# A second transformer block: some weight remainders formed by an accumulating DMA, the residual scaled later and on VectorE, heads normed token tile by token tile, convolution taps queued

## The chip, the cores and the metric

One core of a Trainium2 chip runs the whole program. The engines are PE (TensorE), DVE (VectorE), ACT (ScalarE), POOL (GpSimd) and SP, whose queue here only issues DMAs. The metric is the device time of one execution in microseconds; lower is better.

## The reference

Two blocks follow one another on 512 tokens of width 1024. The first is a mixer, a cross attention and a convolutional feed-forward network; nothing in it changes. The second block, cut to what matters:

```python
h = rms_norm(x, norm1_g)
q, k, v, glu_a, glu_b = split(h @ w_in)          # 8 heads of 64; glu parts 512 wide
q, k = rms_norm per head (gains q_norm_g, k_norm_g)
attn = stick_breaking_attention(q, k, v)         # strictly causal, weights in log space
c = glu_a * sigmoid(glu_b)
c = causal_depthwise_conv(c)                     # 31 taps
c = silu(layer_norm(c))
x = x + concat([attn, c]) @ w_out
x = x + (silu(conv3(gate)) * val) @ w_down       # gate, val = split(rms_norm(x) @ w_up)
```

Here `x` is the first block's output, which ends in an RMS norm of its own (gain `final_norm_g`).

## The kernel before

Every product is made of three: both operands are split into a high part (rounded to the fp32r type that PE reads) and a low part, the remainder, and `mm3` adds high by high, high by low and low by high. Activations lie with features on partitions, 512 tokens on the free axis.

Weights come in 105 planned units of 128 x 2048 values (1 MB) plus three early ones. `prep` loads a unit into `raw`, casts it to `whi` on ACT (L195) and subtracts on DVE to get `wlo` (L196). `raw`, `whi` and `wlo` have two buffers each, so a unit's parts can be formed only when the unit two before it has been used up. In this text a unit has its number in the plan: 60, 61, 62 and 64 are the four column blocks of the gated part (`glu(0)` to `glu(3)`), 63 the second half of the keys, 65 and 66 the values, 67 to 70 the output projection. The three early units (all of the queries, half of the keys) are split ahead of time into slots E, F and G.

`mov_stage` multiplies 128-token tiles by a unit of 512 columns; it fills two pairs of PSUM banks (`pp`) weight half by weight half, so all four token tiles end together. `heads` then norms the heads for two tiles at a time: ACT squares, DVE sums (L731), POOL computes the inverse root (L737 to L740), DVE multiplies (L741), PE transposes (L745), ACT and DVE split the result. Between the products and this norming `heads` calls `gated(2)` or `gated(3)`, which queues the 48 products of a `glu` and a run of taps.

A tap is one DVE instruction on 128 x 512 values (L832). There are 120, in one chain: `conv` orders each behind the one before with `issue_after`. The first block's last norm is applied to the residual `h` by four POOL instructions (L871) before the attention.

The attention goes through pieces (hp, n): head pair 0 to 3, key step 0 to 2. `sticks` forms the scores on PE, then Abs, Exp and Ln on ACT, a maximum-and-add on DVE and a split; `breaks` adds the sums of the blocks behind on PE and takes Exp on ACT (L803); `gather` multiplies by the values. `conv_norm` is the layer norm and Silu of the convolution, and `attended` the half of the output projection that reads the heads.

No engine's order is written by hand: a scheduler places the instructions of each engine when the kernel is built, within the order of the code and the `issue_after` ties, and ACT table loads are put in after that. On the chip each engine goes through its own list in that order.

Of the kernel before, what the change touches and what calls it, by code (L numbers as in the profile page):

```python
# [57 lines left out]


PLAN, EARLY = _plan()  # L60

_SMALL = {}
_n = 0
# [12 lines left out]
def block_kernel(  # L76
# [36 lines left out]
    def col(n):  # L113
        return tp.tile([P, n], F32, tag=f"col{n}", name=f"col{n}", bufs=6 if n == 16 else 8)
# [27 lines left out]
    def over2(ap, n=2):  # L142
        return ap.unsqueeze(1).to_broadcast([P, n, ap.shape[-1]])
# [24 lines left out]
    def half(name, a, b, dt=F32R):  # L168
        return part(slot(name, dt), a, b)
# [4 lines left out]
    def prep(pieces=((0, 8),), before=None, between=None, early=None, slots=None):  # L174

        i = state["next"] if early is None else len(PLAN) + early
        if i == len(PLAN) and early is None:
            return
        if early is None:
            state["next"] += 1  # L180
        _, kind, place = (PLAN + EARLY)[i]
        n = place[2] * 256 if kind == "dwn" else UNIT
        raw = wp.tile([P, UNIT], F32, tag="raw", name="raw")
        hi = slot(slots[0]) if slots else wp.tile([P, UNIT], F32R, tag="whi", name="whi")
        lo = slot(slots[1]) if slots else wp.tile([P, UNIT], F32R, tag="wlo", name="wlo")
        for a, b in pieces:
            cs = slice(a * n // 8, b * n // 8)
            if before:
                before(a, b)
            sp.dma_start(out=raw[:, cs], in_=wts[i][:, cs])  # L190
        for a, b in pieces:
            cs = slice(a * n // 8, b * n // 8)
            if between:
                between(a, b)
            act.copy(hi[:, cs], raw[:, cs])  # L195
            dve.tensor_tensor(lo[:, cs], raw[:, cs], hi[:, cs].bitcast(F32), ALU.subtract)  # L196
        if kind == "hlf":
# [24 lines left out]
    def mov_stage(xh, xl, nt, early=()):  # L222

        pts = [pair() for _ in range((nt + 1) // 2)]
        early = list(early)
        for half in range(2):
            wh, wl = early.pop(0) if early else weights()
            for kk in range(4):
                k = 4 * half + kk
                for t in range(nt):  # L230
                    out = pts[t // 2][:, t % 2, :]
                    st = slice(t * P, (t + 1) * P)
                    mm3(out, xh[:, k, st], xl[:, k, st], wh[:, kk, :], wl[:, kk, :],
                        k == 0, k == KC - 1)
        return pts
# [6 lines left out]
    def par(name, i=0, n=1):  # L242
        o = _SMALL[name][0] + i
        return sm[:, o : o + n]
# [443 lines left out]
    def glu(i):  # L688
        pt = sta_unit(ph, pl)
        if i == 0:  # L690
            norms()
        ab = v3(t4(), 2, 512)
        dve.tensor_tensor(ab, pt, over2(rb2), ALU.mult)
        sig = act.activation(ab[:, 1, :], ab[:, 1, :], AF.Sigmoid)
        if i == 3:
            with tc.issue_after(sig.ins):
                act.preload_act_table_set(tables)
        dve.tensor_tensor(cc[:, i, 30:542], ab[:, 0, :], ab[:, 1, :], ALU.mult)  # L698

    rb2 = rb3 = None  # L700

# [14 lines left out]

    rr, rr2 = keep("rr"), keep("rr2")

    def heads(name, gain, sc, between, early=()):
        gc = col(1)  # L720
        dve.tensor_scalar(gc, par(gain), sc, None, ALU.mult)
        pts = mov_stage(ph, pl, NT, early)
        dst = [half(name + "0", 4, T), half(name + "1", 4, T)]
        between()
        for i in range(2):
            src = pts[i].rearrange("p a (b d) -> p (a b) d", d=HD)
            qn = norm2[:, 2 * i : 2 * i + 2, :]
            heads16 = qn.rearrange("p a (b d) -> p (a b) d", d=HD)
            act.activation(qn, pts[i], AF.Square)
            ms = col(16)  # L730
            dve.tensor_reduce(ms, heads16, AX.X, ALU.add)  # L731
            ms2 = ms.rearrange("p (a b) -> p a b", a=2)

            def per_token(c):
                return c[:, 2 * i : 2 * i + 2].unsqueeze(2).to_broadcast([P, 2, 8])

            pool.tensor_tensor(ms2, ms2, per_token(rr2), ALU.mult)  # L737
            pool.tensor_scalar(ms, ms, EPS, None, ALU.add)
            pool.tensor_tensor(ms, ms, mhalf[:, :16], ALU.pow)  # L739
            pool.tensor_tensor(ms2, ms2, per_token(rr), ALU.mult)  # L740
            dve.tensor_tensor(heads16, src, ms.unsqueeze(2).to_broadcast([P, 16, HD]), ALU.mult)  # L741
            tr = pair().rearrange("p a (b c) -> p (a b) c", b=2)
            for t in range(2):
                for hp in range(4):
                    pe.transpose(tr[:, hp, t * P : (t + 1) * P], qn[:, t, hp * P : (hp + 1) * P], ident)  # L745
            ts = slice(2 * i * P, (2 * i + 2) * P)
            scale_split(dst[0][:, :, ts], dst[1][:, :, ts], tr, gc)
        return dst
# [56 lines left out]
    def gather(hp):  # L805

        o = single(0)
        for n in range(3):
            for a in reversed(STEPS[n]):
                for e in range(2):  # L810
                    hs = slice(e * HD, (e + 1) * HD)
                    vs = slice(hp * P + e * HD, hp * P + (e + 1) * HD)
                    pe.matmul(o[hs, a * P :], v2[:, a, vs], taken(hp, n)[:, e, cols_of(a)],  # L813
                              start=a == 3, stop=a == 0, skip_group_check=True)
        copy_split(qT[0][:, hp, :], qT[1][:, hp, :], o)


    done = [0] * 4
    tap = None

    def conv(n, *chunks):

        nonlocal tap
        for _ in range(n):
            for i in chunks:
                k = done[i]
                done[i] += 1
                if k == 0:
                    identity(cv[:, i, :], cc[:, i, 30:542], scale=par("dw_w", 4 * 30 + i),
                             bias=par("dw_b", i))  # L830
                with tc.issue_after(tap.ins) if tap else nullcontext():
                    tap = dve.scalar_tensor_tensor(  # L832
                        cv[:, i, :], cc[:, i, k : k + 512], par("dw_w", 4 * k + i), cv[:, i, :],
                        ALU.mult, ALU.add)

    norm2 = half("D1", 4, T, F32)
    glu(0)
    split_early(2)
    conv(10, 0)
    turns = {1: ((20, 0, 1),), 2: ((10, 1, 2),), 3: ((20, 2), (30, 3))}  # L840

    def gated(i):
        glu(i)
        for n, *chunks in turns[i]:
            conv(n, *chunks)

    gated(1)
    qT = heads("G", "qg", HD ** -0.5, lambda: gated(2), early[:2])
    kT = heads("F", "kg", 1.0, lambda: gated(3), early[2:])
    v2 = half("E0", 4, T, F32)  # L850
    stk = {}

# [11 lines left out]
    def taken(hp, n):  # L864

        at = (0, 1024 * (hp % 2), 768)[n]
        return part(place(6 if n == 1 else 4 + hp % 2), 2, WIDE[n], at)

    for u in range(4):
        hu = h[:, 2 * u : 2 * u + 2, :]  # L870
        pool.tensor_tensor(hu, hu, over2(rb3), ALU.mult)  # L871

    cl = None
    ch = []
# [66 lines left out]
    def attended(u, after=None):  # L941
        pt = pair()
        half_out(u, qT[0], qT[1], [pt[:, j, :] for j in range(2)], after)
        for j in range(2):
            c = 2 * u + j
            dve.scalar_tensor_tensor(h[:, c, :], h[:, c, :], par("g_fin", c), pt[:, j, :],
                                     ALU.mult, ALU.add)
# [17 lines left out]
    for i, x in enumerate(seq):  # L965

        while todo < len(seq) and todo <= i + 2 and not (x[1] == 2 and seq[todo][1] == 1):
            sticks(*seq[todo])
            todo += 1
        weighted = breaks(*x)  # L970
        if x[1] == 2:
            gather(x[0])
    with tc.issue_after(weighted.ins):
        act.preload_act_table_set("silu_and_others")
    conv_norm()
# [127 lines left out]
```

## Time and profile before

| | us |
|---|---|
| median of 3 runs (1246.56 to 1247.7) | 1246.66 |
| the profiled execution | 1246.8 |
| its span, first to last instruction | 1245.1 |
| PE busy | 1226.2 |
| DVE busy | 771.2 |
| ACT busy | 485.2 |
| POOL busy | 110.0 |

The profiled execution has 1.7 us around its span. An operation is named by line, engine and the tiles out<-in; a line can be a helper's, such as L123 to L125 for the three products of `mm3`. Busy times of PE are those of pipelined matmuls, one of which is shown as 0.39 us while the next starts 0.23 us after it.

### The profile page before, as it was taken

To read this page: it belongs to the slowest core of one execution; us is meant where nothing else is said; L and a number is where in the kernel's file an instruction comes from. 1 tells how busy PE (TensorE), PEld (TensorE's weight loads), DVE (VectorE), ACT (ScalarE), POOL (GpSimd) and SP (SyncE) were. 2 spreads that over 40 slices of the span, in tenths; PEclk is the share of its full clock that TensorE was granted. 3 is DMA by queue.
4 is the path that set the end of the run, shared out by engine and by line. 5 is a ranking of instruction groups with operands and counts; after the bars stand their busy time and mean duration, and the time that the engine had idled before them with its cause. 6 is when DMAs were issued, how large, how long until landed. Compare 5 with 4: busy or idle time off the path is not lost.

```text
span 1245.1 us, 13634 instructions
## 1 busy us (share of the span) xinstructions
PE 1226.2 (98%) x5712; PEld 1009.9 (81%) x5712; DVE 771.2 (62%) x813; ACT 485.2 (39%) x528; POOL 110.0 (9%) x125
## 2 busy tenths in 40 slices
PE   8999999999999999999999899999999999999998
PEld 6889888788888888888888778677888888888887
DVE  7855634744766664466375999985775555346532
ACT  6433424623544342243254125873443333223310
POOL 1100210012000000000054412000400000000000
PEclk9999999999999999999999999999999999999999
DMA  8233332312222222222343012201222233223222
GB/s 275 97 106 131 102 102 68 136 68 101 74 97 102 102 102 102 92 83 97 118 152 135 0 35 68 68 1 68 102 99 81 92 102 102 102 102 102 84 68 86
DMA packets 20445, 118.32 MB, mean 95 GB/s; under 512 B 2208, under 2 KB 4128, under 8 KB 7712
## 3 DMA queue, kind: packets, MB, share of 16 engines
q1 hardware_dynamic: 20096, 117.20, 27.4%
q8 instruction: 44, 0.72, 0.2%
q10 hardware_dynamic: 288, 0.26, 0.1%
q14 instruction: 17, 0.14, 0.0%
HBM read 115.35 MB, written 2.10 MB: 94 GB/s over the span
## 4 chain that ended last, share of the span: by engine, by line
PE 92%; DVE 4%; ACT 2%; issue 1%; POOL 1%; DMA 0%; SPq 0%; DVEq 0%; ACTq 0%
PE pp L125 28%; PE pp L123 28%; PE pp L124 28%; DVE H L832 2%; PE ps L123 1%; PE ps L124 1%; PE ps L125 1%; POOL col L739 0%; PE ps L317 0%; DMA A<-in_xT 0%; PE ps L813 0%; DVE t L785 0%; PE pp L774 0%; ACT t L783 0%; PE pp L745 0%
## 5 line engine op out<-in xcount | busy, mean ns | idle before, releaser
L195 ACT CAST whi<-raw 128x2048 fp32r<-128x2048 f32 (+3 forms) x109 | 197.9, 1817 | 425.7 <-PE pp L124 358.5
L196 DVE TENSOR_TENSOR wlo<-raw,whi 128x2048 fp32r<-128x2048 f32 (+3 forms) x109 | 236.7, 2173 | 71.3 <-ACT whi L195 70.7
L123 PE MATMUL pp<-B,whi 128*128 128x512 f32 x672 | 261.7, 390 | 2.4 <-ACT whi L195 2.4
L125 PE MATMUL pp<-B,wlo 128*128 128x512 f32 x672 | 262.1, 390 | 0.2
L124 PE MATMUL pp<-C,whi 128*128 128x512 f32 x672 | 261.8, 390 | 0.0
L124 PE MATMUL pp<-G,whi 128*128 128x512 f32 x448 | 175.1, 391 | 0.0
L125 PE MATMUL pp<-F,wlo 128*128 128x512 f32 x416 | 162.2, 390 | 0.0
L123 PE MATMUL pp<-F,whi 128*128 128x512 f32 x416 | 161.5, 389 | 0.0
L123 PEld LDWEIGHTS pp<-B,whi 128*128 128x128 f32 x672 | 126.2, 188 | 29.3 <-ACT whi L195 3.3
L125 PEld LDWEIGHTS pp<-B,wlo 128*128 128x128 f32 x672 | 126.1, 188 | 27.8 <-DVE wlo L196 1.5
L124 PEld LDWEIGHTS pp<-C,whi 128*128 128x128 f32 x672 | 126.2, 188 | 26.7 <-issue 0.5
L124 PEld LDWEIGHTS pp<-G,whi 128*128 128x128 f32 x448 | 84.1, 188 | 17.6 <-issue 0.2
L625 DVE TENSOR_TENSOR A<-pp,A 128x1024 f32<-128x1024 f32 x23 | 28.2, 1224 | 105.6 <-PE pp L125 105.6
L646 DVE SCALAR_TENSOR_TENSOR H<-H,sm,H 128x512 f32<-128x512 f32 x132 | 92.8, 746 | 0.7
L125 PEld LDWEIGHTS pp<-F,wlo 128*128 128x128 f32 x416 | 78.1, 188 | 16.4 <-issue 0.2
L123 PEld LDWEIGHTS pp<-F,whi 128*128 128x128 f32 x416 | 78.1, 188 | 16.4 <-issue 0.2
L832 DVE SCALAR_TENSOR_TENSOR H<-H,sm,H 128x512 f32<-128x512 f32 x120 | 90.2, 780 | 1.2
L651 DVE TENSOR_TENSOR H<-pp,rb 128x1024 f32<-128x1024 f32 x22 | 26.8, 1224 | 50.6 <-PE pp L125 44.4
L128 ACT ACTIVATE H<-H,sm 128x512 f32<-128x512 f32 x70 | 54.3, 808 | 7.5 <-DVE H L698 7.5
L997 DVE TENSOR_TENSOR H<-pp,rb 128x512 f32<-128x512 f32 x22 | 15.2, 691 | 60.9 <-PE pp L125 54.7
L123 PE MATMUL pp<-D,whi 128*128 128x512 f32 x112 | 43.6, 389 | 0.0
L124 PE MATMUL pp<-E,whi 128*128 128x512 f32 x112 | 43.6, 389 | 0.0
(293 smaller groups left out, 1797.9 us busy)
## 6 DMA issues: line engine op xcount, KB each, us to landing
raw<-in_wts SPq DMA_DIRECT2D x99, 1024.0 KB, 4.8
raw<-in_wts SPq DMA_DIRECT2D x8, 768.0 KB, 4.0
A<-in_xT SPq DMA_DIRECT2D x3, 512.0 KB, 6.8
out<-A SPq DMA_DIRECT2D x3, 512.0 KB, 2.8
D<-in_memT SPq DMA_DIRECT2D x1, 1024.0 KB, 10.7
raw<-in_wts SPq DMA_DIRECT2D x3, 256.0 KB, 7.0
A<-in_xT SPq DMA_DIRECT2D x2, 256.0 KB, 3.9
raw<-in_wts SPq DMA_DIRECT2D x2, 128.0 KB, 4.1
```

The source lines that it names most:

```text
L123: pe.matmul(out, wh, xh, start=start, stop=False, **kw)
L124: pe.matmul(out, wh, xl, start=False, stop=False, **kw)
L125: pe.matmul(out, wl, xh, start=False, stop=stop, **kw)
L128: act.activation(out, in_, AF.Identity, scale=scale, bias=bias)
L195: act.copy(hi[:, cs], raw[:, cs])
L196: dve.tensor_tensor(lo[:, cs], raw[:, cs], hi[:, cs].bitcast(F32), ALU.subtract)
L625: dve.tensor_tensor(hu, pt, hu, ALU.add)
L646: dve.scalar_tensor_tensor(dst, hs[:, k : k + 512], w(k), dst, ALU.mult, ALU.add)
L651: dve.tensor_tensor(hs[:, :, 2:], pt, over2(rb), ALU.mult)
L832: tap = dve.scalar_tensor_tensor(cv[:, i, :], cc[:, i, k : k + 512], par("dw_w", 4 * k + i), cv[:, i, :], ALU.mult, ALU.add)
L997: dve.tensor_tensor(hs[:, 2:514], pt[:, 0, :], rb, ALU.mult)
```

## The change

Four edits, all in the second block.

- Units 61 to 68 (the list `SUMMED` holds eight) get their low part in another way: ACT writes minus the rounded weight into `wlo` (a copy with scale -1), and a DMA that POOL issues adds `raw` to it in place. The DVE subtraction goes.
- The four POOL instructions that scale `h` go; `attended` scales instead, on DVE, tied behind the last `gather`.
- `heads` goes token tile by token tile: all eight contraction steps of a tile, then its norm. Tiles 0 and 1 lie in the single PSUM banks, 2 and 3 in pairs. It needs both weight units from its first tile on.
- The taps follow one list, `TURNS`, and are handed out in numbers: 8 behind `glu(0)`, 16 behind `glu(1)`, some behind each tile's norm, the rest behind `glu(2)` and `glu(3)`.

```diff
+SUMMED = [i for i, p in enumerate(PLAN) if p[0] == "w_in_2"][1:]
+SUMMED += [i for i, p in enumerate(PLAN) if p[0] == "w_out_2"][:2]
...
-            dve.tensor_tensor(lo[:, cs], raw[:, cs], hi[:, cs].bitcast(F32), ALU.subtract)
+            if early is None and i in SUMMED:
+
+                act.activation(lo[:, cs], raw[:, cs], AF.Copy, scale=-1.0)
+                pool.dma_start(out=lo[:, cs].bitcast(F32), in_=raw[:, cs], accum_op=ALU.add)
+            else:
+                dve.tensor_tensor(lo[:, cs], raw[:, cs], hi[:, cs].bitcast(F32), ALU.subtract)
...
-        pts = mov_stage(ph, pl, NT, early)
+        ws = list(early) + [weights() for _ in range(2 - len(early))]
         dst = [half(name + "0", 4, T), half(name + "1", 4, T)]
+        for t in range(NT):
+            ps = single() if t < 2 else pair()[:, 0, :]
+            st = slice(t * P, (t + 1) * P)
+            for k in range(KC):
+                wh, wl = (w[:, k % 4, :] for w in ws[k // 4])
+                mm3(ps, ph[:, k, st], pl[:, k, st], wh, wl, k == 0, k == KC - 1)
+            qn = norm2[:, t, :]
+            heads8 = qn.rearrange("p (b d) -> p b d", d=HD)
+            act.activation(qn, ps, AF.Square)
+            ms = tp.tile([P, 8], F32, tag="col16", name="col16", bufs=6)
+            dve.tensor_reduce(ms, heads8, AX.X, ALU.add)
+            pool.tensor_scalar(ms, ms, rr2[:, t : t + 1], EPS, ALU.mult, ALU.add)
+            pool.tensor_tensor(ms, ms, mhalf[:, :8], ALU.pow)
+            pool.tensor_scalar(ms, ms, rr[:, t : t + 1], None, ALU.mult)
+            conv(taps[t], dve.tensor_tensor(heads8, ps.rearrange("p (b d) -> p b d", d=HD),
+                                            ms.unsqueeze(2).to_broadcast([P, 8, HD]), ALU.mult))
         between()
...
+    TURNS = [0] * 8 + [0, 1] * 22 + [1, 2] * 8 + [2, 3] * 22 + [3] * 8
...
-    qT = heads("G", "qg", HD ** -0.5, lambda: gated(2), early[:2])
-    kT = heads("F", "kg", 1.0, lambda: gated(3), early[2:])
+    conv(16, glu(1))
+    qT = heads("G", "qg", HD ** -0.5, (0, 4, 4, 8), lambda: conv(8, glu(2)), early[:2])
+    kT = heads("F", "kg", 1.0, (0, 6, 5, 8), lambda: conv(120, glu(3)), early[2:])
...
-    for u in range(4):
-        hu = h[:, 2 * u : 2 * u + 2, :]
-        pool.tensor_tensor(hu, hu, over2(rb3), ALU.mult)
...
         half_out(u, qT[0], qT[1], [pt[:, j, :] for j in range(2)], after)
+        hu = h[:, 2 * u : 2 * u + 2, :]
+        with tc.issue_after(gathered.ins):
+            dve.tensor_tensor(hu, hu, over2(rb3), ALU.mult)
```

What this does to the order on three queues, at the places of which the prediction speaks. Line numbers of the changed kernel are up to ten higher: there L131 is `identity`, L134 the copy of `copy_split`, L142 that of `scale_split`, L198 and L201 the cast and the copy with scale -1, L792 to L794 Abs, Exp and Ln of `sticks`, L813 the Exp of `breaks`, L808 and L811 its products, L823 `gather`, L910 the Silu of `conv_norm`, L978 the table load written in the code.

First ACT between the keys' heads and the first scores, now (D is the tile of the normed heads, F the keys' slot, H the taps' tiles):

```order
L741 ACTIVATE D_4359<-pp 128x512
L201 ACTIVATE wlo<-raw 128x2048
L741 ACTIVATE D_4359<-pp 128x512
L198 CAST whi<-raw 128x2048 x2
L201 ACTIVATE wlo<-raw 128x2048
L142 ACTIVATE F_4797<-pp,col_4788 128x4x256 x2
L702 ACTIVATE t_5003<-t_5003 128x512
L705 ACT_TABLE_LOAD
L131 ACTIVATE H_2138<-H_2137,sm 128x512
L792 ACTIVATE t_5102<-pp 128x768
```

The two casts in one row are those of units 65 and 66; the copy before them is unit 65's, the one behind them unit 66's, and the splits of the keys (L142) stand behind that. Before, the low parts of 65 and 66 were no work of ACT.

Then ACT from the Ln of piece (3,1) to the last Exp of `breaks`. Before (t is a piece's working tile, B, C and E hold weights and split pieces, G the gathered heads):

```order
L783 ACTIVATE t_5558<-t_5558 128x1024
L803 ACTIVATE B_5356<-pp 128x768
L784 ACTIVATE t_5558<-t_5558 128x1024
L803 ACTIVATE E_5282<-pp 128x768
L131 CAST C_5228<-t_5558 128x1024
L888 ACTIVATE t_5626<-H_2138 128x512
L888 ACTIVATE t_5629<-H_2138 128x512
L803 ACTIVATE B_5356<-pp 128x1024
L974 ACT_TABLE_LOAD
L888 ACTIVATE acc<-H_2138 128x512 x2
L131 CAST G_4674<-ps_5608 128x512
```

and now:

```order
L794 ACTIVATE t_5573<-t_5573 128x768
L910 ACT_TABLE_LOAD
L910 ACTIVATE H_2138<-H_2138,sm 128x512 x2
L813 ACT_TABLE_LOAD
L813 ACTIVATE B_5387<-pp 128x768
L910 ACT_TABLE_LOAD
L910 ACTIVATE H_2138<-H_2138,sm 128x512
L134 CAST t_5687<-H_2138 128x512
L134 CAST G_4552<-ps_5553 128x512
L910 ACTIVATE H_2138<-H_2138,sm 128x512
L134 CAST t_5692<-H_2138 128x512
L134 CAST D_5124<-t_5573 128x768
```

and, directly behind these rows:

```order
L792 ACTIVATE t_5589<-pp 128x1024
L134 CAST acc<-H_2138 128x512 x2
L793 ACT_TABLE_LOAD
L793 ACTIVATE t_5589<-t_5589 128x1024
L794 ACT_TABLE_LOAD
L794 ACTIVATE t_5589<-t_5589 128x1024
L813 ACT_TABLE_LOAD
L813 ACTIVATE E_5313<-pp 128x768
L134 CAST C_5259<-t_5589 128x1024
L813 ACTIVATE B_5387<-pp 128x1024
```

Before, one table load stood behind all pieces. Now `conv_norm` lies among the last pieces, and there are six loads from the Ln of (3,1) to the Exp of (3,1) (the row `E_5313<-pp`), where there was none, and a seventh at the end (L978).

Last PE, where the gathered heads meet the output projection. Before, 18 products of unit 67 and the product of the last head pair that reads E:

```order
L124 MATMUL pp<-G_4675,whi 128x512
L125 MATMUL pp<-G_4674,wlo 128x512
L123 MATMUL pp<-G_4674,whi 128x512
L124 MATMUL pp<-G_4675,whi 128x512
L125 MATMUL pp<-G_4674,wlo 128x512
L813 MATMUL ps_5608<-E_5282,E_5051 64x384 x2
L123 MATMUL pp<-G_4674,whi 128x512
L124 MATMUL pp<-G_4675,whi 128x512
```

and now:

```order
L126 MATMUL pp<-G_4552,whi 128x512
L127 MATMUL pp<-G_4553,whi 128x512
L128 MATMUL pp<-G_4552,wlo 128x512
L811 MATMUL pp<-D_5124,negtri 128x384 x2
L808 MATMUL pp<-B_5298,negone 128x256 x2
L808 MATMUL pp<-B_5298,negone 128x128 x2
L811 MATMUL pp<-D_5124,negtri 128x384 x2
L823 MATMUL ps_5639<-E_5313,E_5084 64x384 x2
L126 MATMUL pp<-G_4552,whi 128x512
L127 MATMUL pp<-G_4553,whi 128x512
```

The `gather` product that reads E (the Exp of (3,1)) stood and stands behind 18 products of unit 67, but now the `breaks` products of (3,1) come between, and E comes from behind the table loads. On PE the scores of piece (0,2) also move from behind the projection of the values to within it.

## Rows read from the trace of the kernel before

**Rows 1.** The page, part 1: busy time, share and instructions of each engine.

```profile
PE 1226.2 (98%) x5712; PEld 1009.9 (81%) x5712; DVE 771.2 (62%) x813; ACT 485.2 (39%) x528; POOL 110.0 (9%) x125
```

**Rows 2.** Windows of 50 us: busy time by engine, granted TensorE clock, DMA share, GB/s.

```profile
700.00:750.00 50.00, 44.28 (x193) 36.34 (x192) 47.65 (x62) 9.84 (x9) 14.89 (x13) 0.93 0.11 35
...
800.00:850.00 50.00, 46.57 (x278) 33.71 (x277) 39.77 (x54) 34.88 (x43) 1.01 (x1) 1.00 0.00 1
```

**Rows 3.** Waits of PE over the span: total us, times, longest us.

```profile
PE pp L745 <- DVE D L741: 5.7, 2, 3.6
```

**Rows 4.** PE timeline, 700 to 760: start, us, line, operation, tiles, [idle before].

```profile
709.94 0.39 PE L125 MATMUL pp<-B,wlo 128*128 128x512 f32 x1
...
713.97 1.56 PE L745 MATMUL pp<-ident,D 128*128 128x128 f32 x8 [3.64 <-DVE D L741]
...
717.62 1.94 PE L745 MATMUL pp<-ident,D 128*128 128x128 f32 x8 [2.08 <-DVE D L741]
...
742.10 0.39 PE L123 MATMUL pp<-B,whi 128*128 128x512 f32 x1
...
752.98 0.39 PE L123 MATMUL ps<-whi,B 128*128 128x512 f32 x1
```

**Rows 5.** PE timeline, 755 to 800, within the values' projection.

```profile
756.16 1.04 PE L745 MATMUL pp<-ident,D 128*128 128x128 f32 x8
...
756.95 0.48 PE L125 MATMUL ps<-whi,C 128*128 128x512 f32 x1
...
779.02 0.39 PE L125 MATMUL ps<-whi,C 128*128 128x512 f32 x1
```

**Rows 6.** ACT timeline, 615 to 780.

```profile
652.17 1.92 ACT L195 CAST whi<-raw 128x2048 fp32r<-128x2048 f32 x1 [2.83 <-PE pp L124]
...
682.57 1.15 ACT L694 ACTIVATE t<-t 128x512 f32<-128x512 f32 x2
...
715.57 1.11 ACT L139 ACTIVATE G<-pp,col 128x1024 fp32r<-128x1024 f32 x1 [3.49 <-PE pp L745]
```

**Rows 7.** DVE timeline, 615 to 780.

```profile
686.67 19.41 DVE L832 SCALAR_TENSOR_TENSOR H<-H,sm,H 128x512 f32<-128x512 f32 x21
...
716.24 1.23 DVE L741 TENSOR_TENSOR D<-pp,col 128x1024 f32<-128x1024 f32 x1 [0.44 <-POOL col L740]
...
719.84 2.28 DVE L196 TENSOR_TENSOR wlo<-raw,whi 128x2048 fp32r<-128x2048 f32 x1
...
726.35 14.78 DVE L832 SCALAR_TENSOR_TENSOR H<-H,sm,H 128x512 f32<-128x512 f32 x22
```

**Rows 8.** POOL timeline, 615 to 780.

```profile
680.88 10.95 POOL L871 TENSOR_TENSOR A<-A,rb 128x1024 f32<-128x1024 f32 x4 [8.31 <-ACT rb L338]
...
712.99 2.93 POOL L739 TENSOR_TENSOR col<-col,mhalf 128x16 f32<-128x16 f32 x1
```

**Rows 9.** DMA issues: size of each, median us from issue to landing.

```profile
raw<-in_wts SPq DMA_DIRECT2D x99, 1024.0 KB, 4.8
...
D<-in_memT SPq DMA_DIRECT2D x1, 1024.0 KB, 10.7
```

**Rows 10.** ACT timeline, 770 to 870, the attention's end and what follows.

```profile
820.14 0.85 ACT L784 ACTIVATE t<-t 128x768 f32<-128x768 f32 x1
...
826.11 1.06 ACT L783 ACTIVATE t<-t 128x1024 f32<-128x1024 f32 x1
...
840.22 1.28 ACT L974 ACT_TABLE_LOAD   x1
...
841.52 1.15 ACT L888 ACTIVATE acc<-H 128x512 f32<-128x512 f32 x2
...
855.91 1.52 ACT L909 ACTIVATE H<-H,sm 128x512 f32<-128x512 f32 x2 [5.35 <-DVE H L908]
```

**Rows 11.** PE timeline, 800 to 862: first output product that reads the convolution.

```profile
858.20 0.64 PE L123 MATMUL pp<-t,whi 128*128 128x512 f32 x2
```

**Rows 12.** DVE timeline, 770 to 870: the last tap.

```profile
830.65 0.74 DVE L832 SCALAR_TENSOR_TENSOR H<-H,sm,H 128x512 f32<-128x512 f32 x1
```

More of the change, by code (lines that the diff above doesn't have):

```diff
@@ L697, in glu @@
                 act.preload_act_table_set(tables)
-        dve.tensor_tensor(cc[:, i, 30:542], ab[:, 0, :], ab[:, 1, :], ALU.mult)
+        return dve.tensor_tensor(cc[:, i, 30:542], ab[:, 0, :], ab[:, 1, :], ALU.mult)
     rb2 = rb3 = None
@@ L717, in block_kernel, with heads @@
     rr, rr2 = keep("rr"), keep("rr2")
-    def heads(name, gain, sc, between, early=()):
+    def heads(name, gain, sc, taps, between, early=()):
         gc = col(1)
         dve.tensor_scalar(gc, par(gain), sc, None, ALU.mult)
-        pts = mov_stage(ph, pl, NT, early)
+        ws = list(early) + [weights() for _ in range(2 - len(early))]
         dst = [half(name + "0", 4, T), half(name + "1", 4, T)]
+        for t in range(NT):
[14 more added lines that the diff above has]
+                                            ms.unsqueeze(2).to_broadcast([P, 8, HD]), ALU.mult))
         between()
         for i in range(2):
[L726 to L741, printed above, removed]
             tr = pair().rearrange("p a (b c) -> p (a b) c", b=2)
@@ L744, in heads @@
                 for hp in range(4):
-                    pe.transpose(tr[:, hp, t * P : (t + 1) * P], qn[:, t, hp * P : (hp + 1) * P], ident)
+                    pe.transpose(tr[:, hp, t * P : (t + 1) * P],
+                                 norm2[:, 2 * i + t, hp * P : (hp + 1) * P], ident)
             ts = slice(2 * i * P, (2 * i + 2) * P)
@@ L814, in gather, with conv @@
                               start=a == 3, stop=a == 0, skip_group_check=True)
-        copy_split(qT[0][:, hp, :], qT[1][:, hp, :], o)
+        return copy_split(qT[0][:, hp, :], qT[1][:, hp, :], o)
+    TURNS = [0] * 8 + [0, 1] * 22 + [1, 2] * 8 + [2, 3] * 22 + [3] * 8
     done = [0] * 4
     tap = None
-    def conv(n, *chunks):
+    def conv(n, after=None):
         nonlocal tap
[L824 to L834, printed above, removed]
+        tap = after or tap
+        for _ in range(min(n, len(TURNS))):
+            i = TURNS.pop(0)
+            k = done[i]
+            done[i] += 1
+            if k == 0:
+                identity(cv[:, i, :], cc[:, i, 30:542], scale=par("dw_w", 4 * 30 + i),
+                         bias=par("dw_b", i))
+            with tc.issue_after(tap.ins) if tap else nullcontext():
+                tap = dve.scalar_tensor_tensor(
+                    cv[:, i, :], cc[:, i, k : k + 512], par("dw_w", 4 * k + i), cv[:, i, :],
+                    ALU.mult, ALU.add)
     norm2 = half("D1", 4, T, F32)
-    glu(0)
+    conv(8, glu(0))
     split_early(2)
[L839 to L847, printed above, removed]
-    qT = heads("G", "qg", HD ** -0.5, lambda: gated(2), early[:2])
-    kT = heads("F", "kg", 1.0, lambda: gated(3), early[2:])
+    conv(16, glu(1))
+    qT = heads("G", "qg", HD ** -0.5, (0, 4, 4, 8), lambda: conv(8, glu(2)), early[:2])
+    kT = heads("F", "kg", 1.0, (0, 6, 5, 8), lambda: conv(120, glu(3)), early[2:])
     v2 = half("E0", 4, T, F32)
@@ L971, in block_kernel @@
         if x[1] == 2:
-            gather(x[0])
+            gathered = gather(x[0])
     with tc.issue_after(weighted.ins):
```

## Prediction

> **What bounds the kernel now.** I read the page first, then windows over the second block, then the waits of PE, then the timelines of each engine where those waits lie. The page says that PE is busy for 1226.2 of 1245.1 us [rows 1]: nothing off PE can give more than some 19 us, and a change pays only where PE stands still or works slowly. The windows show two such stretches in the second block: 700 to 750 with 44.3 of 50 us busy and a granted clock of 0.93, and 800 to 850, the attention, with 46.6 [rows 2]. In the first the waits name one line: the transposes of the normed heads wait 5.7 us in two pieces for DVE [rows 3]. In the second the waits are small and scattered, and ACT goes from one pass to the next.
>
> **The heads (the gain).** The products of `glu(2)` end at 709.94 + 0.39 = 710.3. The queries' transposes come after 3.64 us, take 1.56, wait 2.08 more and take 1.94 [rows 4]. The same eight take 0.79 from their start to the next product in the projection, after no wait [rows 5]. So the wait also halves the pace behind it: that is the lower of PE's two levels, 1.2 instead of 2.4 GHz, and the 0.93 of the window. 48 products take 752.98 - 742.10 = 10.9 us [rows 4], so the 96 of the keys take 21.8.
>
> Normed tile by tile, only the last tile's norm is left when its products end, and 10.9 us of `glu(2)` lie over it. What can be late is DVE's queue. ACT ends the Sigmoid of `glu(0)` at about 683.2, then has unit 63's cast and its sign copy (1.9 each, as the cast [rows 6]) and the convolution's start (0.8) before the first tap: 687.8. From there to the last tile's product DVE has 18 taps at 0.67 (14.78 / 22) and nine steps of 0.6 (half the 1.23 of 1,024 columns) [rows 7]: 17.5 us, so 705.3; POOL's root (2.93 for 16 columns [rows 8], half as many now) lies under four of the taps. That is 5 us ahead of 710.3, and without that margin each us late is a us lost. Two sets of transposes then cost 1.6: the keys' products begin at 711.9, end at 733.7 and `glu(3)` ends at 744.6. The keys' transposes no longer lie inside the projection but ahead of it: it begins at 746.2 against 752.98. It took 779.4 - 753.0 = 26.4 us with 1.6 of transposes and the scores of two pieces, so 1.5 a piece; with none and three pieces it takes 26.3. Its end, which I call X, is 772.5 against 779.4 [rows 4, 5]: **6.9 us earlier, with one piece's scores more done**.
>
> **The accumulating DMA.** DVE loses eight subtractions of 2.28 us [rows 7] and ACT gains eight passes of 1.9. Neither is on the path here. What counts is the chain cast, sign copy, transfer, which can begin only when the buffer two units back is free. The trace has no such transfer. A plain load of the same 1 MB lands 4.8 us after its issue, the slowest of that size 10.7 [rows 9]; an addition in place moves at least what a load moves, so it is not shorter than 4.8. I take 9.6, twice the load, since two streams of 1 MB are read, and 10.7 as the other end. Deadlines:
> - Unit 61: cast at 652.17 [rows 6], sign copy done at 655.9. PE begins `glu(0)` at 652.2, and its order needs the low part after 36 + 23 products, at 665.6: 9.7 us.
> - Unit 65: free at 733.7, done at 735.6, needed at 746.4: 10.8 us.
> - Unit 66: free at 744.6, cast and sign copy to 748.5. 26 products (5.9) and the scores of two and a half pieces (3.5) lie ahead of its first use, 755.6: 7.1 us.
> - The others have over 13 us.
>
> So unit 66 comes 2.5 us late (nothing at 4.8; at 10.7 it is 3.6 with 1.0 at unit 61). I count 1.2 of it, as DVE goes on with taps meanwhile and ACT later waits less for DVE. The Trainium skill, "Collectives: The Full Stack", section "The bandwidth ceiling: the fold count and why AG ≠ RS ≠ AR", says that an add in the DMA path needs two source reads where a copy has one, which halved the rate of a reduction. By the plain load's row the transfer would take 4.8 us and the sum below would be 1248.7, by this rule 9.6 and 1249.9; no run here shows the transfer yet.
>
> **POOL and the residual.** The 10.95 us of POOL beside the taps slowed them: 21 took 19.41, 0.92 each [rows 7, 8]. That helps DVE, which does not bound. The four scalings on DVE (1.2 each, 4.9) come behind the last `gather`, ahead of the steps that free PSUM for the output products. 36 products, 8.2 us, cover them; without the cover they would cost 4.9.
>
> **The attention (where I expect the gain to go).** DVE ended the taps at 831.4 [rows 12]. Without its eight subtractions (18.2), POOL's slowing (21 x 0.25 = 5.3) and with 7 us from the heads it ends them near 801, and the order has `conv_norm` among the last pieces. Before, ACT ended the Ln of piece (3,1) at 821.0, 41.6 after X [rows 10]. Now three passes of (0,2) are done ahead of X (-3.1), the four squares of `conv_norm` are added (2.3, [rows 10]), so are two sign copies (3.8), and I allow 1.0 for a block of 13 taps ahead of a maximum: 45.6, so 818.1. Of the 6.9 us, 2.9 are left.
>
> Then comes the wall: in order on ACT to the Exp of (3,1) six table loads of 1.28 (7.7), four Silus of 0.76 (3.0), four copies of 0.57 (2.3), two copies of PE results (1.2), two Exps of 768 columns (1.5), and Abs, Exp and Ln of 1,024 (3.1) [rows 10]: 18.8 us as durations, 18.5 with their overlaps. The Exp of (3,1) ends at 836.6. PE has some 9 us of products to do meanwhile (the scores of (3,2), 18 products of unit 67, the `breaks` of two pieces), then stands still before the `gather` product that reads it. Behind that it needs 0.5 for it, 17 products (3.9), the `breaks` of (3,2) (2.0), its Exp and `gather` (1.6) and 60 products (13.6): 21.6 us, so the products on the heads end at 858.2. Before they ended at 858.20, where the products on the convolution begin [rows 11]. **The gain of the heads is spent here to the last tenth.** The long stand, about 7 us, should halve PE's pace behind it; at the heads 5.7 us of waits cost 2.7 more, so I count 2.0.
>
> **Sum.** 0.0 + 1.2 + 2.0 = +3.2 on the profiled execution's 1246.8, or 1250.0. That execution is 0.14 above the median, so **1249.9**. 0.2% (2.5 us) is about what a measurement of this kernel can tell from no change.
>
> **Rivals.**
> - *The wall costs what the heads give, and no more* (no late unit, pace kept after the stand): 1246 to 1248.5. For it: PE's pace recovers within a few products, and 9.6 us is a guess. 0.22.
> - *Faster: ACT reaches the wall sooner.* After DVE's last tap, near 801, no pass of ACT stands behind a tap any more. If the Ln of (3,1) ends by 813.5, 4.6 us sooner than I sum, and neither unit 66 nor the pace behind the stand costs anything, the end is 1249.9 - 4.6 - 1.2 - 2.0 = 1242.1; with those two gone it decides at 815.6, 2.5 us sooner than I sum. Against it: by the durations the passes alone make some 41 of the 45.6 us. 0.25.
> - *The addition is much slower than two loads*, for instance three (14.4): units 61, 65 and 66 are 4.7, 3.6 and 7.3 us late, and the end is near 1262. Only DMA engines that stand mostly idle speak against it. 0.10.
> - *A table switch costs more than its load.* Here the load takes 1.28 and the next pass starts 1.30 after it [rows 10], so I sum 1.28. If ACT also had to drain before each load, as much again, six loads would add 7.7 and the end is near 1257. 0.06. The Trainium skill, "ScalarE: Activation LUTs", section "What ACT_TABLE_LOAD costs", states such a drain: about 1.28 us for the load and 1.38 for the drain, which for six loads would be 8.3 us more; the trace's one load among running passes does not agree.
>
> The forecast itself has 0.37; its own range is 1248 to 1253, and of the 0.37 I put 0.10 within 0.2%. So faster 0.25, same 0.32, slower 0.43. The range reaches from the faster rival to the drain: 1241.5 to 1257.
>
> **What the changed profile would show.** Right: no wait of the transposes for DVE near 710; the projection's first product near 746; eight POOL issues of 1 MB landing after some 9 us, and a wait of 1 to 4 us for unit 66's low part near 755; taps ended near 800; seven table loads from about 818 on; a stand of PE of 5 us or more ahead of a `gather` product near 830 to 837, and transposes or products at double spacing behind it. Wrong: if PE's idle time at the attention's end is under 3 us, the wall was covered and the result is faster; if unit 61 or 65 makes PE wait, the addition is slower than I took; if a load is followed by more than 0.2 us of standing still, it has a drain.

## The result, and the profile after

| | before | after |
|---|---|---|
| median of 4 runs each, us | 1246.68 | 1257.38 (1255.06 to 1258.63) |
| after / before, 95% interval | | 1.0082 (1.0066 to 1.0098) |
| the profiled execution, its span | 1246.8, 1245.1 | 1255.06, 1253.4 |

The change makes the kernel 0.8% slower, where 0.26% was forecast: 1257.38 us lies above the forecast's own range of 1248 to 1253 and at the upper end of the whole range, 1257. The profiled execution happens to be the shortest of the four; it is 8.3 us above that of before. A second set of the same kernel beside the last experiments gave 1256.19 and 1.0076 (1.0063 to 1.0090), with a profile of 1256.9 us span, to which I return.

The page's line of busy times, and windows with granted clock, of after (to read against [rows 1, 2]):

```profile
PE 1231.0 (98%) x5712; PEld 1013.8 (81%) x5712; DVE 749.2 (60%) x817; ACT 507.5 (40%) x546; POOL 114.1 (9%) x137
```

```profile
700.00:750.00 50.00, 50.00 (x239) 41.85 (x238) 48.04 (x71) 18.54 (x16) 21.47 (x20) 1.00 0.33 85
...
780.00:790.00 10.00, 7.26 (x53) 4.47 (x54) 10.00 (x16) 8.65 (x12) 0.00 (x0) 0.99 0.93 276
790.00:800.00 10.00, 10.00 (x52) 7.66 (x51) 9.86 (x14) 6.67 (x9) 0.00 (x0) 0.67 0.01 2
...
823.00:842.00 19.00, 11.05 (x52) 7.49 (x50) 6.87 (x9) 18.84 (x22) 0.10 (x1) 0.80 0.00 1
```

The same 10 us of before, for the third of these rows:

```profile
790.00:800.00 10.00, 9.17 (x59) 6.17 (x59) 9.89 (x14) 8.76 (x12) 0.00 (x0) 1.00 0.01 2
```

In the window 700 to 750 PE is now busy all the time at a clock of 1.00: the stretch that was the worst is cured. The loss lies further on, in two places. From 790 to 800 PE is busy but slow, 0.67 where before had 1.00. From 823 to 842 ACT is busy for 18.84 of 19 us and PE for 11.05.

PE's four longest waits after 772, and its timeline. The wait for the heads' transposes of [rows 3] is not among them, and the values' projection (`ps<-whi,B`) starts at 746.19 where [rows 4] had 752.98:

```profile
PE ps L823 <- ACT E L813: 5.8, 1, 5.8
PE pp L126 <- ACT B L813: 2.2, 1, 2.2
PE pp L808 <- DVE B L135: 2.1, 1, 2.1
PE ps L823 <- ACT B L813: 1.1, 1, 1.1
```

```profile
746.19 0.48 PE L126 MATMUL ps<-whi,B 128*128 128x512 f32 x1
...
779.91 0.91 PE L784 MATMUL pp<-G,F 64*128 64x256 f32 x12
...
789.44 0.33 PE L808 MATMUL pp<-B,negone 128*128 128x128 f32 x1 [2.14 <-DVE B L135]
...
794.81 1.54 PE L784 MATMUL pp<-G,F 64*128 64x256 f32 x12
...
841.44 1.55 PE L823 MATMUL ps<-E,E 128*64 128x384 f32 x4 [5.80 <-ACT E L813]
...
866.43 0.39 PE L126 MATMUL pp<-t,whi 128*128 128x512 f32 x1
```

The same twelve score products take 0.91 us at 779.91 and 1.54 at 794.81, behind the waits near 787 and 789: the lower of PE's two levels, 1.2 instead of 2.4 GHz. The last row is the first product that reads the convolution, the landmark of [rows 11]: 866.43 against 858.20. That is 8.2 of the 8.3 us, so everything happens ahead of it.

ACT from the Ln of piece (3,1) to the Exp of (3,1), which PE waits for:

```profile
821.70 0.84 ACT L794 ACTIVATE t<-t 128x768 f32<-128x768 f32 x1
822.56 1.28 ACT L910 ACT_TABLE_LOAD   x1
823.86 1.52 ACT L910 ACTIVATE H<-H,sm 128x512 f32<-128x512 f32 x2
825.40 1.28 ACT L813 ACT_TABLE_LOAD   x1
826.69 0.81 ACT L813 ACTIVATE B<-pp 128x768 f32<-128x768 f32 x1
827.52 1.28 ACT L910 ACT_TABLE_LOAD   x1
...
834.55 1.28 ACT L793 ACT_TABLE_LOAD   x1
...
836.92 1.28 ACT L794 ACT_TABLE_LOAD   x1
...
839.28 1.28 ACT L813 ACT_TABLE_LOAD   x1
840.58 0.81 ACT L813 ACTIVATE E<-pp 128x768 f32<-128x768 f32 x1
```

This is the wall: 822.54 to 841.39, 18.85 us, in which ACT is never idle.

### The profile page after: what moved, and what is told of

It reads as the page before. It is cut to its first block, busy times and chain, and to the rows that moved or that the text cites. A ratio compares the mean times of both kernels' runs of the same rounds, so it can differ in the third digit from the quotient of the medians.

```text
span 1253.4 us, 13674 instructions
## 1 busy us (share of the span) xinstructions
PE 1231.0 (98%) x5712; PEld 1013.8 (81%) x5712; DVE 749.2 (60%) x817; ACT 507.5 (40%) x546; POOL 114.1 (9%) x137
## 4 chain that ended last, share of the span: by engine, by line
PE 87%; DVE 6%; ACT 4%; POOL 2%; issue 1%; DMA 0%; SPq 0%; DVEq 0%; POOLq 0%; ACTq 0%
PE pp L128 27%; PE pp L127 27%; PE pp L126 27%; DVE H L845 4%; POOL col L745 1%; PE ps L126 1%; PE ps L127 1%; PE ps L128 1%; POOL col L744 1%; PE ps L325 0%; PE ps L823 0%; PE pp L808 0%; PE pp L811 0%; DMA A<-in_xT 0%; ACT t L792 0%
## 5 line engine op out<-in xcount | busy, mean ns | idle before, releaser
L198 ACT CAST whi<-raw 128x2048 fp32r<-128x2048 f32 (+3 forms) x109 | 197.9, 1817 | 420.5 <-PE pp L127 338.3
L204 DVE TENSOR_TENSOR wlo<-raw,whi 128x2048 fp32r<-128x2048 f32 (+3 forms) x101 | 219.3, 2173 | 66.2 <-ACT whi L198 65.7
L654 DVE SCALAR_TENSOR_TENSOR H<-H,sm,H 128x512 f32<-128x512 f32 x132 | 92.8, 747 | 0.7
L633 DVE TENSOR_TENSOR A<-pp,A 128x1024 f32<-128x1024 f32 x23 | 28.2, 1224 | 105.4 <-PE pp L128 105.4
L845 DVE SCALAR_TENSOR_TENSOR H<-H,sm,H 128x512 f32<-128x512 f32 x120 | 83.2, 744 | 2.8 <-ACT H L131 2.5
L131 ACT ACTIVATE H<-H,sm 128x512 f32<-128x512 f32 x70 | 54.2, 808 | 4.6 <-DVE H L706 4.6
```

The source lines that it names most:

```text
L633: dve.tensor_tensor(hu, pt, hu, ALU.add)
L654: dve.scalar_tensor_tensor(dst, hs[:, k : k + 512], w(k), dst, ALU.mult, ALU.add)
L845: tap = dve.scalar_tensor_tensor(cv[:, i, :], cc[:, i, k : k + 512], par("dw_w", 4 * k + i), cv[:, i, :], ALU.mult, ALU.add)
```

## The experiments

For every kernel the same landmarks are read from the timelines of PE and ACT: X is the end of the values' projection, "Ln" and "Exp" those of piece (3,1), and "end" is the start of the first product on the convolution. Each ratio is against the kernel before on the same chip; the medians of different rows can come from different chips.

| kernel | X | X to Ln | Ln to Exp | Exp to end | end | table loads from 815 on | median us | ratio, 95% interval |
|---|---|---|---|---|---|---|---|---|
| before | 779.4 | 41.6 | 8.5 | 28.7 | 858.2 | 1 | 1246.68 | |
| after | 772.7 | 49.8 | 18.9 | 25.0 | 866.4 | 7 | 1257.38 | 1.0082 (1.0066 to 1.0098) |
| after, second profile | 772.8 | 52.6 | 18.8 | 25.8 | 870.0 | 7 | 1256.19 | 1.0076 (1.0063 to 1.0090) |
| Silus late | 772.6 | 49.5 | 9.9 | 29.0 | 861.0 | 1 | 1250.68 | 1.0029 (1.0019 to 1.0038) |
| norm late | 772.7 | 46.5 | 8.8 | 39.1 | 867.1 | 1 | 1257.63 | 1.0086 (1.0071 to 1.0101) |
| output units subtracted | 771.7 | 51.9 | 15.1 | 25.3 | 863.9 | 5 | 1250.70 | 1.0034 (1.0021 to 1.0048) |
| all units subtracted | 772.3 | 51.4 | 12.1 | 29.2 | 865.0 | 3 | 1253.17 | 1.0047 (1.0032 to 1.0062) |
| scaling on POOL early | 777.5 | 48.8 | 18.8 | 25.1 | 870.3 | 7 | 1258.65 | 1.0089 (1.0074 to 1.0104) |
| Silus late, taps paced by 5 | 772.8 | 45.9 | 9.1 | 27.1 | 854.8 | 1 | 1245.90 | 0.9996 (0.9986 to 1.0006) |
| Silus late, scaling on POOL late | 772.0 | 49.6 | 15.5 | 23.1 | 860.1 | 1 | 1248.88 | 1.0016 (1.0007 to 1.0026) |
| the two above together | 772.3 | 45.4 | 10.5 | 27.1 | 855.3 | 1 | 1245.68 | 0.9993 (0.9984 to 1.0003) |
| Silus late, paced by 6 | 773.0 | 47.2 | 10.8 | 28.2 | 859.2 | 1 | 1247.83 | 1.0005 (0.9997 to 1.0014) |
| Silus late, paced by 5, output units subtracted | 773.1 | 47.5 | 8.9 | 27.1 | 856.6 | 1 | 1244.72 | 0.9981 (0.9972 to 0.9990) |
| Silus late, paced by 6, output units subtracted | 772.4 | 49.1 | 7.5 | 30.5 | 859.5 | 1 | 1250.01 | 1.0022 (1.0012 to 1.0031) |

**Silus late.** Only the four Silus move.

```diff
-            act.activation(ci, ci, AF.Silu, scale=par("ln_g", i), bias=par("ln_b", i))
+            with tc.issue_after(weighted.ins):
+                act.activation(ci, ci, AF.Silu, scale=par("ln_g", i), bias=par("ln_b", i))
```

> The changed kernel with only the four Silus of conv_norm held behind the last Exp of the attention, so that ACT loads one table there instead of seven; sums, squares and root stay where they are. Theory 1, the wall of loads and Silus between the Ln and the Exp of piece (3,1) (18.9 us in the changed kernel) is what the change costs: the Exp of (3,1) follows its Ln after some 6 us, PE's stand of 5.8 us goes, and PE then has only its own 29.6 us of work left behind 825.2, so the products on the heads end near 854.9 instead of 866.4: 1243 to 1246 us. Theory 2, the attention ahead of the wall is late for other reasons (taps ahead of the maxima, sign copies, passes of conv_norm) and the loads lie beside waits that would be there anyway: PE's waits move to other lines and the time stays at 1252 us or more.

The time falls by 6.7 us, from 1257.38 to 1250.68: neither number given, between the two. The wall is 9.9 us instead of 18.9, and the stand of 5.8 is gone. But the end comes 5.4 earlier, not 11.5. Two waits that the wall had covered are now on the path, and PE's waits name them (the 2.1 us stand in the changed kernel too):

```profile
PE pp L126 <- DVE A L951: 2.5, 1, 2.5
PE pp L808 <- DVE B L135: 2.1, 1, 2.1
PE pp L126 <- ACT G L134: 1.4, 1, 1.4
```

The Silus are put ahead of the cast of the last `gather`, and the late scalings on DVE, tied behind that `gather`, run from 845.66 to 850.28: here their cover of products is too short. So theory 1 holds for the wall, and theory 2 is right too: the attention ahead of it stays at 49.5.

**Norm late.** The first sums of `conv_norm` are tied on PE behind the last product of `breaks`.

```diff
-                    pe.matmul(out, negtri, s[:, e, cols_of(a)], start=False, stop=i == 1,
+                    state["last"] = pe.matmul(out, negtri, s[:, e, cols_of(a)], start=False, stop=i == 1,
...
-            mm = pe.matmul(mu, ones, cv[:, i, :], start=i == 0, stop=i == 3)
+            with tc.issue_after(state["last"].ins):
+                mm = pe.matmul(mu, ones, cv[:, i, :], start=i == 0, stop=i == 3)
```

> The changed kernel with the whole of conv_norm begun behind the last product of breaks, as it lay in the kernel before. Theory 1 (loads and Silus alone): as with the Silus held, 1243 to 1246, or a little more where the convolution's products wait for the Silus, since the norm takes some 22 us from its first product to its last cast. Theory 2 (conv_norm's sums, squares and root inside the attention cost as well, about 2.3 us of ACT, 6 of DVE and 4 of PE): it is faster than the kernel with the Silus held by 2 us or more, unless the convolution's products wait: 1240 to 1243.

The time misses the numbers of both, and what comes is what both had set aside, a wait of the convolution's products. The attention loses 3.0 us (46.5 against 49.5): in these two profiles that is what the norm's sums and squares cost inside it. But from Exp to the end it takes 39.1. The scalings now run in the middle of the norm, between its squares and its sum on DVE, and PE waits:

```profile
PE ps L897 <- DVE t L892: 7.6, 1, 7.6
```

**Output units subtracted.** Units 67 and 68 leave `SUMMED`.

```diff
-SUMMED += [i for i, p in enumerate(PLAN) if p[0] == "w_out_2"][:2]
```

> The changed kernel with the two units of the output projection, 67 and 68, taken out of the accumulating DMA: their lower parts are subtracted on DVE again. ACT loses two sign copies of 1.9 us just ahead of the attention's passes, DVE gains two subtractions of 2.28, and by its order ACT loads five tables instead of seven. If the sign copies delay the attention: 3 to 4 us faster, 1253 to 1254. If only loads count: two loads of 1.28 fewer, 2.6 us faster, about 1255. If DVE's queue ahead of the maxima is what delays the attention: 0 to 4 us slower, 1257 to 1261.

1250.70, below all three numbers. In the profile the wall is 3.8 us shorter: two loads stand in it where six stood, but ACT also waits in it now. X to Ln is 2.1 longer: taking two sign copies off ACT and putting two subtractions on DVE does not shorten the attention. The end is 2.5 earlier, as for two loads fewer; the medians differ by 6.7. The profiled execution, 1252.58, is one of two with a granted clock near 0.990 over the whole span (0.990 and 0.991); the three at 0.994 or 0.995 took 1250.21 to 1250.70, so this profile does not stand for the median.

**All units subtracted.** `SUMMED = []`.

> The changed kernel with no unit left to the accumulating DMA: all eight lower parts are subtracted on DVE again, heads, taps and late scaling stay as changed. DVE gains 18.2 us, ACT loses 15.2, no 1 MB additions. By its order ACT loads three tables around the attention's end instead of seven. If loads set the loss: at least as good as with the two output units alone taken out (1250.7), 1246 to 1251. If the additions relieve a DVE that bounds the heads and the attention: later taps, late maxima, waits of the heads' transposes, 1253 to 1260.

1253.17, at the edge of the second range, and two of the three things named there come. The heads' transposes do not wait, and X is 0.5 earlier: with eight more subtractions on DVE the heads and the projection are as early as with the transfers. But the taps end at 815.2 instead of 802.9, PE waits for maxima in the attention, which it does not do in the changed kernel's first profile, and X to Ln is 1.6 longer:

```profile
PE pp L807 <- DVE t L794: 1.5, 2, 1.3
```

So the DMA form shortens nothing ahead of X. In the attention it may be worth something: in all four pairs of profiles that differ by this alone (these two edits against the changed kernel, and the last two rows of the table against the same forms with the DMA) X to Ln is 1.6 to 2.1 longer with subtractions on DVE. These are single profiles, and the changed kernel itself was read at 49.8 and at 52.6, so it is not shown; the times of these two edits are shorter all the same. From Ln on only one Silu block still cuts in, ahead of the Exp of (3,2).

**Scaling on POOL early.** The four scalings stand ahead of the attention on POOL again, as before the change.

> The changed kernel with the residual's four scalings back on POOL, ahead of the attention, beside the taps. My theory: the scalings late on DVE (4.6 us in the changed kernel, near 854 to 859) are covered by products, no wait of PE names them, so nothing is gained, and POOL slows the taps beside it by some 5 us: 1257 to 1260. Rival: the late scalings hold up the steps that free PSUM: 2 to 4 us faster, 1253 to 1255.

Within the first range, but the place is another. The scalings hold POOL from 680.12 to 690.53, and the DMA issue and the first head norms stand behind them; the last keys are normed late and PE waits 0.8 and 1.3 us. The projection starts only 0.4 us later but ends 4.8 later: 1.3 of wait lies inside it, and from 756 to 766, behind that wait, the granted clock is 0.66 where the changed kernel had 1.00. Moving the scalings away from there is a needed part of the heads' gain, which I had not counted.

**Taps paced.** With the Silus late, the last 44 taps are queued five behind the subtraction of each piece.

```diff
-    kT = heads("F", "kg", 1.0, (0, 6, 5, 8), lambda: conv(120, glu(3)), early[2:])
+    kT = heads("F", "kg", 1.0, (0, 6, 5, 8), lambda: conv(9, glu(3)), early[2:])
...
-        copy_split(*blk(hp, n), ex)
+        sub = copy_split(*blk(hp, n), ex)
+        if (hp, n) != (0, 0):
+            conv(5, sub)
```

> The kernel with the Silus held late (1250.7), and the last 44 taps not queued at once but five behind the subtraction of each piece of the attention. In the changed kernel and in the one with the Silus held the attention takes 49.8 and 49.5 us from the end of the values' projection to the Ln of (3,1), where before it took 41.6 and I summed 45.6. Theory: blocks of taps on DVE (99% busy from 773 to 803) ahead of the maxima make it long, and so halve PE's pace near 790; then with five taps a piece it takes 44 to 47, and the time is 1245 to 1249, unless the norm, which now starts later, makes the convolution's products wait. Rival: ACT's passes with two sign copies and the squares make it long; then it stays at 49 to 50 and the time at 1250 or more.

1245.90 and 45.9 us, as the theory said. But its reason is mostly another. Paced taps end at 827.7 instead of 802.7, so the norm falls out of the attention by itself; against "norm late", which has blocks of taps and no norm there, the pacing gives 0.6 us (46.5 to 45.9). And the slow stretch stays, near the lower level (window, columns as above):

```profile
790.00:800.00 10.00, 8.95 (x41) 6.87 (x42) 10.00 (x13) 6.35 (x9) 0.00 (x0) 0.54 0.01 2
```

**Scaling on POOL late**, behind the norm's root, Silus behind the cast of the last `gather`. The cut shows the scaling; the rest of the edit names the root and the cast, so that they can be tied to.

```diff
-        with tc.issue_after(gathered.ins):
-            dve.tensor_tensor(hu, hu, over2(rb3), ALU.mult)
+        with tc.issue_after(state["pow"].ins):
+            pool.tensor_tensor(hu, hu, over2(rb3), ALU.mult)
```

> The kernel with the Silus held late (1250.7), with the four residual scalings on POOL behind the norm's root, so that neither taps nor DVE's late steps meet them, and the Silus queued behind the cast of the last gather on ACT. There PE waited 2.5 us for DVE's late step and 1.4 for that cast. If those two waits are a real loss: the products on the heads end 4 to 5 us earlier, near 856, and the time is 1245.5 to 1247.5. If the waits only move (convolution's products then wait for the Silus): 1249 to 1251.

1248.88, 1.8 better and between the two ranges. The two waits are gone, a new one came: beside POOL's scalings (816.99 to 827.51) a subtraction on DVE took 3.11 us, and PE waited 1.8 us for it.

```profile
816.99 10.52 POOL L951 TENSOR_TENSOR A<-A,rb 128x1024 f32<-128x1024 f32 x4
```

```profile
819.86 3.11 DVE L135 TENSOR_TENSOR B<-t,B 128x768 fp32r<-128x768 f32 x1
822.89 2.47 DVE L912 TENSOR_TENSOR H<-H,ps 128x512 f32<-128x512 f32 x4
825.28 0.94 DVE L795 SCALAR_TENSOR_TENSOR t<-pp,t 128x768 f32<-128x768 f32 x1
```

**Both together.**

> The changed kernel with Silus behind the last cast, scalings late on POOL, and taps paced five a piece: the two edits before this one together. If both losses are real and separate: 1240 to 1244, below the kernel before. If the taps' pacing pushes the norm so late that the convolution's products wait for it: 1246 or more.

1245.68, in neither range: with paced taps the scaling's place makes no difference (1245.90 without it). The gains do not add up.

**The changed kernel again, and three more forms.** Six taps a piece is `conv(2, glu(3))` and `conv(6, sub)`.

> The changed kernel unaltered, beside the next three on the same chip: its first four executions spread from 1255.06 to 1258.63 us, and the profiled one was the shortest. No theory says otherwise than 1255 to 1259; the taps in blocks, the wall of loads and PE's stand of 5.8 us should be found again in its trace.

As expected. Its profile shows the same waits within 0.6 us, yet X to Ln is 52.6 against 49.8. What differs is PE's level: 0.54 in 790 to 800 against 0.67. The score products at 794.81 and 794.88 begin together in the two profiles; the profile shows no wait of PE between them and the next scores, which come at 803.14 in the first profile and at 805.10 in the second:

```profile
803.14 0.80 PE L784 MATMUL pp<-G,F 64*128 64x384 f32 x6
```

```profile
794.88 1.54 PE L784 MATMUL pp<-G,F 64*128 64x256 f32 x12
...
805.10 0.80 PE L784 MATMUL pp<-G,F 64*128 64x384 f32 x6
```

> The kernel with Silus late and taps paced (1245.9), with six taps a piece instead of five, two ahead of the pieces: all taps are done one or two pieces sooner, near 820 instead of 827.7. There the norm's root met the late scalings on DVE and PE waited 1.3 us for a half of the norm's result. If the norm's lateness is what is left at the end: 1243 to 1245.5. If six taps a piece hold up the maxima again: the attention takes 47 to 49 us instead of 45.9, and the time is 1247 or more.

1247.83, slower than with five: PE waits 2.8 us for maxima, as the second theory says.

```profile
PE pp L810 <- DVE t L795: 2.8, 2, 1.6
```

My first theory could not be tested in this form: with only two taps queued ahead, 51 taps at six still end behind the ninth piece, at 829.0.

> The kernel with Silus late and taps paced (1245.9), with units 67 and 68 subtracted on DVE instead of added by DMA: two sign copies of 1.9 us fewer on ACT, two subtractions of 2.28 more on DVE, which in that kernel has 8 us idle between 773 and 803. If the sign copies hold up ACT's first passes (as I summed, 3.8 us): Ln of (3,1) 2 to 4 us earlier after the end of the values' projection, 1242 to 1244.5. If DVE's queue still decides: equal or up to 3 us slower, 1245.5 to 1249.

1244.72, the lowest of all these kernels, 0.19% below before (0.10 to 0.28). It is the best of twelve, and its interval overlaps that of the form with the DMA (0.9986 to 1.0006), so which of the two is faster is open. The reason given for it failed: the attention is 1.6 us longer, not shorter. The profile's end (856.6) is not earlier than with the units added by DMA (854.8), so where the median's 1.2 us would come from is open too.

> Six taps a piece and the two output units subtracted on DVE, Silus late. If sign copies and a late norm are both real losses: 1240 to 1243.5, faster than the kernel before by more than 0.2%. If DVE decides, both edits load it between the maxima: 1247 or more.

1250.01, as the second case said: six taps a piece and two more subtractions are too much for DVE between the maxima. Of PE's waits for DVE the longest in the attention names a subtraction (`L812 <- DVE D L134`, 1.9 us); those for the maxima are 0.2.

## Why the prediction was right in direction and short in size

Measured on the profiled execution, the forecast of the end was 858.2 + 1.2 + 2.0 = 861.4, and it came at 866.4. The differences, step by step:

- **The heads' gain: right.** Projection at 746.19 (746.2 forecast), X at 772.7 (772.5), no wait of the transposes. All kernels with the new heads have it, except with the scaling on POOL early.
- **The accumulating DMA: too long, and of no account.** It lands after 7.0 us, not 9.6, and the one late unit cost 0.6 us of a wait of PE's weight load at 755.64, none of PE itself, against the 1.2 that I counted; X shows none of it.

```profile
wlo<-raw POOLq DMA_DIRECT2D x8, 1024.0 KB, 7.0
```

```profile
PEld ps L127 <- DMA wlo<-raw: 0.6, 1, 0.6
```

- **The attention: the step that failed.** "45.6, so 818.1" was 49.8, so 822.5. The taps ended at 802.9 (801 forecast), so the norm did fall into the attention. Of the 4.2 us too few, 0.7 are the norm, which costs 3.0 and not the 2.3 of its squares alone. The blocks of taps cost 0.6 where I allowed 1.0, and 0.3 lies between the profile of after and that with the Silus late. What is left is 3.6 us: with neither norm nor blocks the attention still takes 45.9, where 41.6 - 3.1 + 3.8 makes 42.3. These 3.6 us are no work of ACT: from X to Ln it is busy for 38.8 us in that kernel (taps paced by 5) and for 38.35 before, 0.4 more for the 0.7 that I summed, though only one of the two sign copies lies behind X (774.36; the other starts at 769.80). What grew is ACT's standing still, from 3.2 to 7.1 us, and of the waits that the profile names there 6.1 us are for PE (3.2 before) and 0.6 for DVE (0.6 before). The longest:

```profile
799.75 0.81 ACT L815 ACTIVATE E<-pp 128x768 f32<-128x768 f32 x1 [2.95 <-PE pp L813]
```

So the sum changed only ACT's passes, and left out that ACT would wait longer for PE. In the same place PE runs at 0.54 in that kernel and at 0.67 in the changed one from 790 to 800, where before it ran at 1.00; 10 us at 0.67 to 0.54 are 3.3 to 4.6 us of pace lost. I had granted the attention full pace. That lost pace reaches ACT is seen in the two profiles of the changed kernel, where the scores at 803.14 and 805.10 are followed by their Abs at 804.34 and 806.30. That the clock is all of the 3.6 us fits in size and place, but every kernel with the new heads has 0.50 to 0.80 there, so no run kept the clock up with the early projection, and it is not shown. All these are single profiles, and the changed kernel itself was read at 49.8 and at 52.6: the 0.6 and the 0.7 are no more than readings, while the norm's 3.0 came at a lower clock (0.90 against 0.93 in 750 to 800), which speaks for it.
- **The wall: right.** 18.85 us measured for 18.5, and taken away by one edit (9.9). No load has a drain: in the rows of the wall an engine pass ends at 822.54, the load starts at 822.56, lasts 1.28, and the Silu starts 1.30 after it. The Trainium skill, "ScalarE: Activation LUTs", section "What ACT_TABLE_LOAD costs", adds 1.38 us of drain to each switch; for these seven loads the trace does not agree.
- **Behind the Exp of (3,1):** 25.0 for 21.6 + 2.0. The pace behind PE's stand cost about 1.8 of the 2.0: the `gather` took 1.5 for 0.5 and the 17 products 4.7 for 3.9. The 1.4 too few lie in the `breaks` of (3,2), 2.9 for 2.0, and in its Exp and `gather`, 2.1 for 1.6, in which PE waits 1.1:

```profile
851.67 1.08 PE L823 MATMUL ps<-B,E 128*64 128x512 f32 x4 [1.11 <-ACT B L813]
```

- **The scalings on DVE: covered, but only just.** In the changed kernel nothing waits for them; with the Silus late, where the wall is gone, PE waits 2.5 for the steps behind them. With the taps paced as well, it does not.

So the end is late by 4.4 (the Ln: 4.2 and 0.2 of X) + 0.35 (wall) + 1.4 (behind it) - 1.2 (the unit) = 5.0. Of the two terms that made the forecast slower, the pace came and the unit did not; the direction came out right because the attention and the wall took the heads' gain and more, and most of the size that was missing is the attention's. Of the rivals, the table switch with drain ends nearest (1257), but for the wrong reason: no drain is there, and it is luck that the whole range, which had its upper end from this rival, reaches about as far as the result. The rival "faster" asked for the Ln by 815.6; it came seven us later, and even without norm and blocks at 818.6.

## What to carry to other kernels

Work that comes earlier is not free: a chain that ends sooner lets what hangs on it (here the norm with its Silus) start in a place where it breaks up another function's run on ACT. When something upstream gets faster, ask for each of its readers where it will now be put, and tie the ones that switch tables behind the run that they would cut. The 7 us won on PE at the heads were lost until the queues of ACT and DVE behind them had been spaced again, and then at most 2.5 of them (0.19%) came through, about what a measurement of this kernel can tell from no change.

## What the runs showed of the hardware

- DVE operations with two inputs in SBUF lasted about as long as one of POOL's multiplications (2.6 to 2.7 us each in the mean) when they ran beside them; those with one input in PSUM kept their time. Beside the late scalings a subtraction of 768 columns took 3.11 us (0.96 behind them, at 828.94), while the operations right behind it that read PSUM took their usual 0.94 and 2.47 for four. In the kernel before, the first two of the 21 taps at 686.67 took 2.90 and 2.77 us, and the 19 behind POOL's end took the usual time; the 0.92 each that I read in [rows 7] is a mean of the two kinds, and its sum stands. The Trainium skill, "GPSIMD Engine Reference", section "1. Specifications", names such contention for two SBUF inputs; the trace agrees.
- An accumulating DMA of 1 MB within SBUF lands after 7.0 us (median of eight, 6.9 to 8.9), against 4.8 for a load of that size from the weights' memory, 1.46 times as long. By the Trainium skill, "Collectives: The Full Stack", section "The bandwidth ceiling: the fold count and why AG ≠ RS ≠ AR", an add in the DMA path reads two sources, and a reduction ran at half the rate of a copy; here, on another route and with POOL as issuer, less than that was lost.
- From 750.81 to 822.56 Exp and Ln alternate on ACT without a load between them, but behind the Silu the Exp, the Ln and the next Exp each got a load of their own (834.55, 836.92, 839.28).
- The same program with the same waits had PE at 0.67 in one profile and 0.54 in another in the same 10 us, and differed by 2.8 us in the attention (X to Ln).
- A wait of PE can cost more behind it than it lasts. With the scaling on POOL early, waits of 0.8 us just ahead of the values' projection and 1.3 us within it are followed by ten us at 0.66, where the changed kernel has neither, and the projection takes 4.5 us longer.
- Executions of one kernel differ with the granted clock of their whole span. With the Silus late and the taps paced by 5, six at 0.996 took 1244.9 to 1246.3 us, one at 0.994 took 1247.25, and three at 0.993 took 1248.6 to 1249.1.
